# Placing the value products of two attention branches by TensorE's other work instead of by steps

## The chip, the cores and the metric

One NeuronCore of a Trainium2 chip runs the whole kernel in one launch. The metric is the device time of that launch in microseconds (us). A profiled execution leaves a trace with the time of each instruction on the five engines: TensorE (PE, with its weight loads as PEld), VectorE (DVE), ScalarE (ACT), GpSimd (POOL) and SyncE (SP), which here issues nearly all DMAs, in the order in which they stand on its queue.

## What is computed

The reference is one layer of a streaming encoder with two attention branches. 2048 new frames of one stream (and 128 of eight running streams, which a later part of the kernel serves from caches) are projected, go through both branches, and are merged. Cut to the parts that matter here:

```python
def diff_attention(q, k, v, qpos, kpos, lam):          # branch A: 4 heads of 128
    s = einsum('bhcqk', q, k) * (HEAD_DIM_A ** -0.5)   # c: two score maps
    p = softmax(where(chunk_mask, s, -inf), axis=-1)
    w = p[:, :, 0] - lam * p[:, :, 1]
    return einsum('bhqk,bkhe->bqhe', w, v)

def stick_breaking_attention(q, k, v, qpos, kpos):     # branch B: 8 heads of 64
    z = einsum('bhqk', q, k) * (HEAD_DIM_B ** -0.5)
    log_1m = where(kpos < qpos, log_sigmoid(-z), 0.)
    log_a = log_sigmoid(z) + reverse_cumsum(log_1m) - log_1m
    return einsum('bhqk,bkhd->bqhd', where(kpos < qpos, exp(log_a), 0.), v)
```

Both end in a product of attention weights with values. These value products are what the change moves.

## The kernel before

**Units and steps.** The attention part runs over 8 units, u = 0 to 7. Even units are one head of branch A, odd units two heads of branch B. A unit has 17 steps: first the tile of the running streams (`NT`, only projected here), then the tiles t = 0 to 15 of 128 queries each. Tile t attends to t + 1 blocks of 128 keys, so a step grows with t.

**What a step holds.** In step n the program writes out three streams. The first is a run of projection pieces (`project`, L430 and after: two 128x512 matmuls a piece at L445, for the gates at L521), which are some tiles ahead of the attention. The second is the scores of tile t (`scores`, L651): a chunk is 128 queries by up to 512 keys, two matmuls into one of three PSUM banks `ps_s` (L661, L662) and on the diagonal a third that adds the mask (L665). The third is the value products. `interleave` (L95) spreads the streams evenly over the step. The order in which the program is written is then turned into an order for each engine by a scheduler that lets an instruction pass another one that would have to wait; the engines keep that order.

**From scores to weights.** In B, ScalarE takes two sigmoids of each chunk (L123), VectorE runs a scan over it (L638), which frees the PSUM bank; when a segment of up to eight key blocks is complete, GpSimd multiplies (L644), ScalarE makes a 16-bit copy (L594), VectorE the rest (L595). In A, VectorE evacuates the chunk with a running maximum (L580) and ScalarE takes the exponentials when all chunks of the tile are there. Both end in `turn` (L586): one DMA transpose on SP's queue (L602) writes the segment's weights, turned, into a buffer `wt`. There are five such buffers (`WT_BUFS`); the sixth transpose waits until the products of the first have been read. A unit of A makes 24 such segments, one of B 48, 288 in all.

**B's q and k** are turned by DMA transposes on the same queue (L542, L543), A's by TensorE (L547, L551).

**The value products** (`pv`, L725): for a key block, A takes three matmuls (L718, L719, L720), B two (L722, L723), with the turned weights as stationary operand. Those of step n are written out in step n + 2 (`PV_LAG` = 2), spread over the stretch 0.1 to 1.0 of that step (`V_LO`, `V_HI`), one block at a time among scores and projections.

Of the kernel before, what the change touches and what calls it, by code (L numbers as in the profile page):

```python
# [32 lines left out]
NT = SEQ // P  # L33
# [3 lines left out]
NEG = -3.0e38  # L37
STICK = 14
SEG = 8
PV_LAG = 2  # L40
WT_BUFS = 5
SC_BUFS = 6
V_LO, V_HI = 0.1, 1.0
W_READY = 9
WIDE_BUFS = 6
P0_AT = 2.0, 4.0, 6.0
# [45 lines left out]
    return c  # L92


def interleave(*streams):  # L95

    order = []
    for i, pieces in enumerate(streams):  # L100
        lo, hi = 0.0, 1.0
        if isinstance(pieces, tuple):
            pieces, lo, hi = pieces
        total = sum(cost for cost, _ in pieces) or 1.0
        done = 0.0
        for j, (cost, fn) in enumerate(pieces):
            order.append((lo + (hi - lo) * (done + cost / 2) / total, i, j, fn))
            done += cost
    for _, _, _, fn in sorted(order, key=lambda e: e[:3]):
        fn()  # L110


# [1 line left out]
def layer_kernel(ctx: ExitStack, tc: tile.TileContext, a: dict):  # L114
# [81 lines left out]
    def bank(tag, dt=F32):  # L196
        return ps.tile([P, 512 if dt == F32 else 1024], dt, tag=tag, name=f"ps_{tag}", bufs=BANKS[tag])
# [98 lines left out]
    def split(hi, lo, src, s, on=None):  # L296

        if on is S:
            S.activation(out=hi, in_=src, func=AF.Identity, scale=s)  # L299
        elif on is G:  # L300
            G.tensor_scalar(out=hi, in0=src, scalar1=s, scalar2=0.0, op0=ALU.mult, op1=ALU.add)
        else:
            V.tensor_scalar(out=hi, in0=src, scalar1=s, scalar2=None, op0=ALU.mult)
        V.scalar_tensor_tensor(out=lo, in0=src, scalar=s, in1=hi, op0=ALU.mult, op1=ALU.subtract)
# [282 lines left out]
    def turn(job, seg, scale=None):  # L587

        nb = seg["hi"] - seg["lo"]
        nk = nb * P  # L590
        w16 = seg["n"].bitcast(F16)
        hi, lo, src = w16[:, 0:nk], w16[:, nk : 2 * nk], seg["p"][:, 0:nk]
        if scale is None:
            S.copy(out=hi, in_=src)  # L594
            V.tensor_tensor(out=lo, in0=src, in1=hi, op=ALU.subtract)  # L595
        else:
            split(hi, lo, src, scale, S)
        if job["t"] == NT:
            seg["wt"] = job["pool"].tile([P, 10, P], F16, tag="dwt", name="dwt", bufs=2)
        else:  # L600
            seg["wt"] = wtp.tile([P, 2 * SEG, P], F16, tag="wt", name="wt", bufs=WT_BUFS)
        nc.sync.dma_start_transpose(out=seg["wt"][:, 0 : 2 * nb, :], in_=w16[:, 0 : 2 * nk])  # L602

    def softmax_pair(job):

        segs = job["segs"]
        nm = tiny.tile([P, 2], F32, tag="nm", name="nm")
        V.tensor_reduce(out=nm, in_=job["mx"][:, :, 0 : job["nch"]], axis=AX.X, op=ALU.max, negate=True)
        l = tiny.tile([P, 2, 2], F32, tag="l", name="l")
        for i, seg in enumerate(segs):  # L610
            nk = (seg["hi"] - seg["lo"]) * P
            for c in range(2):
                w = seg[("p", "n")[c]][:, 0:nk]
                act(out=w, in_=w, func=AF.Exp, bias=nm[:, c : c + 1], accum_out=l[:, c, i : i + 1])
        r = tiny.tile([P, 3], F32, tag="r", name="r")
        sums = l[:, :, 0]
        if len(segs) > 1:
            V.tensor_tensor(out=sums, in0=l[:, :, 0], in1=l[:, :, 1], op=ALU.add)
        V.reciprocal(out=r[:, 0:2], in_=sums)
        V.scalar_tensor_tensor(out=r[:, 2:3], in0=sums[:, 0:1], scalar=r[:, 1:2], in1=nlam, op0=ALU.mult, op1=ALU.mult)  # L620
        V.tensor_tensor(out=r[:, 0:1], in0=r[:, 0:1], in1=ls[:, 0:1], op=ALU.mult)
        for seg in segs:
            nk = (seg["hi"] - seg["lo"]) * P
            p, n = seg["p"][:, 0:nk], seg["n"][:, 0:nk]
            V.scalar_tensor_tensor(out=p, in0=n, scalar=r[:, 2:3], in1=p, op0=ALU.mult, op1=ALU.add)
            turn(job, seg, r[:, 0:1])
# [81 lines left out]
    def store(U, t, o):  # L708
        ui = (U["h"] + 4 * U["kind"]) * P
        if U["kind"] == 0:  # L710
            sum_squares(o, P, osums[:, t, U["h"] : U["h"] + 1])
        load(out=o_d[t][:, ui : ui + P], in_=o)

    def pv_block(job, seg, po, wj, vt, first, last):

        wt, nb, c = seg["wt"], seg["hi"] - seg["lo"], job["c"]
        if job["U"]["kind"] == 0:
            T.matmul(po[:, 0:P], wt[:, wj, :], vt[:, :, 0, :], start=first, stop=False)  # L718
            T.matmul(po[:, 0:P], wt[:, wj, :], vt[:, :, 1, :], start=False, stop=False)  # L719
            T.matmul(po[:, 0:P], wt[:, nb + wj, :], vt[:, :, 0, :], start=False, stop=last)  # L720
        else:
            T.matmul(po[:, c * P : (c + 1) * P], wt[:, wj, :], vt[:, c, :, :], start=first, stop=False)  # L722
            T.matmul(po[:, c * P : c * P + 64], wt[:, nb + wj, :], vt[:, c, 0, :], start=False, stop=last)  # L723

    def pv(job):  # L725

        U, t, c = job["U"], job["t"], job["c"]
        segs = job["segs"] if U["kind"] == 0 else job["segs"][::-1]
        order = [(seg, j) for seg in segs for j in range(seg["hi"] - seg["lo"])]

        def block(i):
            seg, j = order[i]
            if i == 0 and (U["kind"] == 0 or c == 0):
                U["po", t] = bank("o")
            pv_block(job, seg, U["po", t], j, U["v"][seg["lo"] + j], i == 0, i == len(order) - 1)
            if i == len(order) - 1 and (U["kind"] == 0 or c == 1):
                store(U, t, natural(U, t, U.pop(("po", t))))

        return [(1.5, lambda i=i: block(i)) for i in range(len(order))]

    def cache_column(name, h):
        return "ab".index(name[0]) * 4 + h
# [167 lines left out]
    steps = [(u, t) for u in range(8) for t in [NT] + list(range(NT))]  # L910
    back = []
    spare, cached = norms()
    jobs = []


    line = []
# [32 lines left out]
    def position(x):  # L949

        m = min(int(x), len(steps) - 1)
        return starts[m] + (starts[m + 1] - starts[m]) * (x - m)

    def take(target, need):

        i = at[0]
        out = []
        while i < len(line) and (i < target or any(m <= need for m, _ in line[i : i + 14])):
            out.append((1.0, line[i][1]))
            i += 1  # L960
        at[0] = i
        return out
# [7 lines left out]
    def duration(t):  # L970
        return SAMPLE_TIME if t == NT else TILE_TIME + (t + 1) / 4
# [3 lines left out]
    with tc.tile_pool(name="p0", bufs=1) as p0:  # L975
# [5 lines left out]
        def wide_tile():  # L981
            return p0.tile([P, KT, 256], F32, tag="wide", name="wide", bufs=WIDE_BUFS)
# [21 lines left out]
        first = wide_tile().rearrange("p k n -> p (k n)")  # L1004
# [207 lines left out]
    cuts = None  # L1212
# [98 lines left out]

        return [branch_weight for _ in branch_weights] + [rest] + [lambda t=t: first(t) for t in tiles[0:2]]

    for n in range(len(steps) + PV_LAG):
        made, qk, vs = [], [], []
        if n < len(steps):
            u, t = steps[n]
            past += duration(t)
            if t == (3 if u == 0 else NT) and u < 7:
                back += prepare_unit(u + 1)  # L1320
            if u == 7 and not back and not spare and not cached and len(branch_weights) > 1:
                branch_weight()
            for fn in back[: -(-len(back) // max(1, (W_READY if u else W_READY + 2) - t % NT))]:
                back.pop(0)()
            for todo, here in ((spare, norm_at), (cached, keys_at)):
                if todo and here(u, t):
                    left = sum(here(*step) for step in steps[n:])
                    for _ in todo[: -(-len(todo) // left)]:
                        todo.pop(0)()
            if t < NT:  # L1330
                qk = scores(units[u], t, made)
        if n >= PV_LAG:
            for job in jobs[n - PV_LAG]:
                vs += pv(job)
        target = position(len(steps) * past / whole + LEAD)
        pieces = take(target, min(n + 1, len(steps) - 1))
        if at[0] == len(line) and not pieces and not spare and not cached:
            if cuts is None:
                cuts = early_work()
            pieces = [(1.0, fn) for fn in cuts[: -(-len(cuts) // (len(steps) + PV_LAG - n))]]  # L1340
            del cuts[: len(pieces)]
        interleave(pieces, qk, (vs, V_LO, V_HI))
        jobs.append(made)
    c01.close()


    with ExitStack() as c2:
# [7 lines left out]
        vs = scales(total(add_up_all(csums), 8), res, "s_c", 8)  # L1355
# [147 lines left out]
```

## Time and profile before

| what | value |
|---|---|
| median of 3 runs | 2333.5 us (2331.74 to 2335.74) |
| the profiled execution, its own time | 2332.17 us |
| its span in the trace | 2330.4 us |
| TensorE busy | 2089.3 us, 90% |
| VectorE, ScalarE, GpSimd busy | 1695.3, 1618.7, 693.9 us |
| mean granted TensorE clock | 0.961 |

The span is the time from the first to the last instruction of the trace; the execution's own time is 1.8 us longer. Busy time of TensorE is the union of its matmuls, whose ends are modelled. An idle time is put down to what ended it: "PE ps_o L722 <- DMA wt<-sc_n" is time in which TensorE stood before a value product of B until the transposed weights had landed.

### The profile page before, as it was taken

Reading aid. Unit: us, or ns where it says so; the run is one execution under the profiler, and the core shown is the slowest. Engines: PE = TensorE matmul, PEld = TensorE weight load, DVE = VectorE, ACT = ScalarE, POOL = GpSimd, SP = SyncE. Lnnn points to the kernel's source line nnn. Section 1 sums busy time; section 2 is a strip of 40 time slices with the busy share of each in tenths; the row PEclk is TensorE's granted clock in tenths of the full one; section 3 lists DMA queues with packets and bytes.
Section 4 is the critical chain, followed back from the end, with each engine's and each line's share of the span. In section 5 each row is a group of like instructions: output and inputs, shape, how many; then the busy total and the mean of one; then the engine's idle time right before and its main releaser. Section 6 shows DMA issues by size and latency. Waiting matters only on the chain. (4 is left out here: it accounts for less than half of the span.)

```text
span 2330.4 us, 41287 instructions
## 1 busy us (share of the span) xinstructions
PE 2089.3 (90%) x14344; PEld 1111.3 (48%) x14344; DVE 1695.3 (73%) x3659; ACT 1618.7 (69%) x3228; POOL 693.9 (30%) x610
## 2 busy tenths in 40 slices
PE   5998899988989888899998888999998688899998
PEld 3654454444545444455554444555454344344443
DVE  4658758669877776998668669777778768776763
ACT  4968767777877677878667777866778556555551
POOL 1222015346310333743024356401334312111211
PEclk7999999999999999999999999999998899899999
DMA  9777659898797899979889899676878899878431
GB/s 330 273 214 205 151 138 220 213 202 192 177 258 168 206 220 210 203 184 235 201 183 221 187 219 224 165 172 151 170 157 181 192 266 224 225 208 222 153 105 47
DMA packets 862402, 458.65 MB, mean 197 GB/s; under 512 B 593930, under 2 KB 801082, under 8 KB 861680
## 3 DMA queue, kind: packets, MB, share of 16 engines
q1 hardware_dynamic: 861244, 455.63, 80.6%
q8 instruction: 112, 1.84, 0.3%
q14 instruction: 98, 0.80, 0.1%
q10 hardware_dynamic: 948, 0.39, 0.1%
HBM read 228.82 MB, written 86.02 MB: 135 GB/s over the span
## 5 line engine op out<-in xcount | busy, mean ns | idle before, releaser
L644 POOL TENSOR_TENSOR sc_p<-sc_p,sc_n 128x127 f32<-128x127 f32 (+7 forms) x192 | 311.3, 1625 | 511.4 <-DVE sc_n L638 495.6
L445 PE MATMUL ps_mm<-wb,hs 128*128 128x512 f16 x1734 | 448.6, 385 | 4.6 <-DMA hs<-hT_d 4.6
L445 PEld LDWEIGHTS <-hs 128*128 128x128 f16 x3120 | 275.7, 99 | 263.6 <-DMA hs<-hT_d 12.7
L445 PE MATMUL ps_mm<-wa,hs 128*128 128x512 f16 x1386 | 349.0, 380 | 6.6 <-DMA hs<-hT_d 6.6
L661 PE MATMUL ps_s<-k,qst 128*128 128x512 f16 (+3 forms) x640 | 228.3, 357 | 72.3 <-DVE sc_n L638 57.5
L638 DVE TENSOR_TENSOR_SCAN sc_n<-ps_s,sc_n,zero_t 128x512 f32<-128x512 f32 x192 | 245.5, 1278 | 46.1 <-ACT ps_s L123 42.0
L595 DVE TENSOR_TENSOR sc_n<-sc_p,sc_n 128x128 f16<-128x128 f32 (+7 forms) x192 | 205.7, 1076 | 49.9 <-ACT sc_n L594 49.6
L521 PE MATMUL ps_t<-wb,hs 128*128 128x512 f16 x918 | 232.4, 380 | 0.0
L662 PE MATMUL ps_s<-k,qst 128*128 128x512 f16 (+3 forms) x640 | 228.0, 357 | 0.0
L722 PE MATMUL ps_o<-v,wt 128*128 128x128 f16 x1088 | 193.6, 228 | 37.9 <-DMA wt<-sc_n 37.8
L123 ACT ACTIVATE sc_p<-ps_s,usc 128x512 f32<-128x512 f32 (+3 forms) x320 | 204.4, 639 | 30.8 <-PE ps_s L662 17.2
L521 PEld LDWEIGHTS <-hs 128*128 128x128 f16 x1632 | 144.5, 99 | 140.5 <-issue 10.1
L594 ACT CAST sc_n<-sc_p 128x128 f16<-128x128 f32 (+7 forms) x192 | 154.3, 809 | 76.5 <-POOL sc_p L644 76.0
L123 ACT ACTIVATE ps_s<-ps_s,usc 128x512 f32<-128x512 f32 (+3 forms) x328 | 199.5, 608 | 0.0
L521 PE MATMUL ps_t<-wa,hs 128*128 128x512 f16 x714 | 187.7, 391 | 6.8 <-ACT qst L554 6.0
L1417 PE MATMUL ps_o<-wo,wa 128*128 128x512 f16 x816 | 182.8, 380 | 2.1 <-ACT wo L299 1.3
L723 PE MATMUL ps_o<-v,wt 128*128 128x64 f16 x1088 | 174.9, 200 | 0.0
L722 PEld LDWEIGHTS <-wt 128*128 128x128 f16 x1088 | 108.9, 103 | 120.7 <-DMA wt<-sc_n 46.6
L723 PEld LDWEIGHTS <-wt 128*128 128x128 f16 x1088 | 106.7, 102 | 73.1 <-issue 2.2
L580 DVE TENSOR_SCALAR_CACHE_REDUCE sc_n<-ps_s,usc 128x512 f32<-128x512 f32 (+3 forms) x160 | 106.3, 665 | 44.6 <-PE ps_s L665 21.7
L580 DVE TENSOR_SCALAR_CACHE_REDUCE sc_p<-ps_s,usc 128x512 f32<-128x512 f32 (+3 forms) x160 | 106.2, 664 | 26.4 <-PE ps_s L662 24.3
L718 PE MATMUL ps_o<-v,wt 128*128 128x128 f16 x544 | 105.0, 225 | 22.8 <-DMA wt<-sc_n 22.4
(365 smaller groups left out, 4346.4 us busy)
## 6 DMA issues: line engine op xcount, KB each, us to landing
hs<-hT_d SPq DMA_DIRECT2D x130, 512.0 KB, 4.5
g_d<-gt SPq DMA_DIRECT2D x68, 256.0 KB, 3.4
wb<-g_d SPq DMA_DIRECT2D x34, 512.0 KB, 5.3
out_dram<-pr SPq DMA_DIRECT2D x204, 64.0 KB, 2.3
wa<-in_w_in_dram SPq DMA_DIRECT2D x34, 256.0 KB, 3.9
o_d<-o SPq DMA_DIRECT2D x136, 64.0 KB, 2.6
hs<-o_d SPq DMA_DIRECT2D x17, 512.0 KB, 7.0
out_dram<-x SPq DMA_DIRECT2D x17, 512.0 KB, 2.8
```

The costliest lines, as they stand in the source:

```text
L123: i = S.activation(**kw)
L445: T.matmul(box["p"], box["h"][:, hi, k, :], U["w"][k][:, wi, :], start=(n == 0), stop=(n == 3 * KT - 1))
L521: T.matmul(box["g"][:, 0:gw], box["h"][:, hi, k, :], U["wg"][k // per][:, k % per, wi, :], start=(j == 0), stop=(j == 3 * KT - 1))
L580: V.tensor_scalar(out=dst[:, lo : lo + n], in0=p[:, 0:n], scalar1=sc_pos, scalar2=None, op0=ALU.mult, op1=ALU.max, accum_out=job["mx"][:, ...
L595: V.tensor_tensor(out=lo, in0=src, in1=hi, op=ALU.subtract)
L638: V.tensor_tensor_scan(out=dst[:, lo : lo + n][:, ::-1], data0=src[:, 0:n][:, ::-1], data1=zero_t[:, 0:1].to_broadcast([P, n]), initial=fi ...
L644: G.tensor_tensor(out=p[:, 0:m], in0=p[:, 0:m], in1=n[:, 1 : m + 1], op=ALU.mult)
L661: T.matmul(p[:, 0:n], qst[:, c, :], kk[:, c, 0:n], start=True, stop=False)
L662: T.matmul(p[:, 0:n], qst[:, 2 + c, :], kk[:, c, 0:n], start=False, stop=not diag)
L722: T.matmul(po[:, c * P : (c + 1) * P], wt[:, wj, :], vt[:, c, :, :], start=first, stop=False)
L723: T.matmul(po[:, c * P : c * P + 64], wt[:, nb + wj, :], vt[:, c, 0, :], start=False, stop=last)
L1417: T.matmul(po, st["y"][:, yi * 8 + k, :], wo[j * 4 + k // 2][:, wi, k % 2, :], start=(n == 0), stop=(n == 3 * KT - 1))
```

## The change

`pv` is no longer called two steps later. `turn` calls it for one segment right after it has written out that segment's transpose, and puts the segment's blocks into a list `due`, each with the mark `spent + 30.0`. `spent` adds up the estimated TensorE time of all that has been written out: 0.44 for a projection piece, 0.22 times its weight for a score chunk, 0.17 for a block of A, 0.085 for one of B. `give` writes out pieces and scores in the evenly mixed order, and after each of them all products whose mark has been reached. All blocks of a segment have the same mark, so they come in one run, where before they were spread over a step. At the end of the attention part what is left in `due` is mixed with the last pieces. The order of the blocks within a tile, the instructions and their number, the buffers and the PSUM banks are the same.

```diff
-PV_LAG = 2
+PV_LAG = 30.0
+PIECE, CHUNK, PV_A, PV_B = 0.44, 0.22, 0.17, 0.085
-V_LO, V_HI = 0.1, 1.0
...
         nc.sync.dma_start_transpose(out=seg["wt"][:, 0 : 2 * nb, :], in_=w16[:, 0 : 2 * nk])
+        if job["t"] < NT:
+            cost = (PV_A, PV_B)[job["U"]["kind"]]
+            due.extend((spent[0] + PV_LAG, cost, fn) for fn in pv(job, seg))
...
-    def pv(job):
+    def pv(job, seg):
...
-        return [(1.5, lambda i=i: block(i)) for i in range(len(order))]
+        return [lambda j=j: block(j) for j in range(nb)]
+
+    def give(order, costs):
+
+        for i, weight, fn in order:
+            fn()
+            spent[0] += weight * costs[i]
+            while due and due[0][0] <= spent[0]:
+                _, cost, product = due.pop(0)
+                product()
+                spent[0] += cost
...
-        if n >= PV_LAG:
-            for job in jobs[n - PV_LAG]:
-                vs += pv(job)
...
+            if n == len(steps) + 1:
+                pieces += [(PV_B / PIECE, fn) for _, _, fn in due]
+                due.clear()
-        interleave(pieces, qk, (vs, V_LO, V_HI))
-        jobs.append(made)
+        give(interleaved(pieces, qk), (PIECE, CHUNK))
```

Lines after the change stand a few lower: the products of B are L726 and L727, their transposes L603, the load of a tile's input L423.

**TensorE, the first products of tile 1 in unit 3 (B).** `wt` are the turned weights, `v` the values, `ps_o` the output's bank; `qst` and `k` belong to the scores of tile 2, `hs` is the input of a projection. Before:

```order
L662 LDWEIGHTS qst_8779
L662 MATMUL ps_s_9229<-k_8515,qst_8779 128x384
L665 LDWEIGHTS idb_194
L665 MATMUL ps_s_9229<-masks_196,idb_194 128x128
L722 LDWEIGHTS wt_9137
L722 MATMUL ps_o_9308<-v_8396,wt_9137 128x128
L723 LDWEIGHTS wt_9137
L723 MATMUL ps_o_9308<-v_8396,wt_9137 128x64
```

After:

```order
L522 LDWEIGHTS hs1_181
L522 MATMUL ps_t_9447<-wb1_1427,hs1_181 128x512
L726 LDWEIGHTS wt_9083
L726 MATMUL ps_o_9502<-v_8404,wt_9083 128x128
L727 LDWEIGHTS wt_9083
L727 MATMUL ps_o_9502<-v_8404,wt_9083 128x64
```

The products stood right behind the scores of tile 2; now they stand among the projections of a later tile. Between the last score matmul of tile 1 and its first product there were 90 matmuls for the first head and 44 for the second; now there are 172 and 183.

**SP, the transposes of q for tile 9 in unit 3.** `wt` with 16 rows are weights of eight key blocks (of tile 7 here), with 2 rows of one block (tile 8); `k` and `qst` are the keys and queries of tile 9. Before:

```order
L602 DMA_TRANSPOSE wt_9877<-sc_n_9841 128x16x128
L602 DMA_TRANSPOSE wt_9939<-sc_n_9906 128x16x128
L602 DMA_TRANSPOSE wt_10034<-sc_n_9980 128x2x128
L525 DMA g_d9_105<-gt0_1421 128x512
L542 DMA_TRANSPOSE k_9920<-k16_9965 128x2x128
L543 DMA_TRANSPOSE qst_10087<-qbuf1_214 128x4x128
```

After:

```order
L603 DMA_TRANSPOSE wt_9868<-sc_n_9825 128x16x128
L543 DMA_TRANSPOSE k_9914<-k16_9947 128x2x128
L716 DMA o_d5_67<-o_9985 128x128
L526 DMA g_d9_105<-gt0_1421 128x512
L544 DMA_TRANSPOSE qst_10083<-qbuf1_214 128x4x128
L603 DMA_TRANSPOSE wt_9931<-sc_n_9891 128x16x128
```

The queries stood behind three transposes of weights; now they stand behind one of these, and ahead of the second.

**SP, the weights of tiles 1 and 2 in unit 3.** `hs` are inputs of later projections, `wt` with 4 rows the weights of tile 1 (one for each head), with 6 rows those of tile 2. Before:

```order
L602 DMA_TRANSPOSE wt_9137<-sc_n_9130 128x4x128
L712 DMA o_d0_62<-o_9245 128x128
L501 DMA out_4_dram<-pr_9295 128x128
L602 DMA_TRANSPOSE wt_9161<-sc_n_9154 128x4x128
L502 DMA out_5_dram<-pr_9295 128x128
L422 DMA hs2_182<-hT_d1_58 128x2048
L542 DMA_TRANSPOSE k_9225<-k16_9298 128x2x128
L543 DMA_TRANSPOSE qst_9425<-qbuf1_214 128x4x128
```

After:

```order
L423 DMA hs2_182<-hT_d1_58 128x2048
L543 DMA_TRANSPOSE k_9168<-k16_9233 128x2x128
L544 DMA_TRANSPOSE qst_9396<-qbuf1_214 128x4x128
L423 DMA hs0_180<-hT_d2_59 128x2048
L603 DMA_TRANSPOSE wt_9107<-sc_n_9100 128x4x128
L526 DMA g_d5_101<-gt0_1421 128x512
L603 DMA_TRANSPOSE wt_9155<-sc_n_9148 128x6x128
L603 DMA_TRANSPOSE wt_9184<-sc_n_9177 128x6x128
```

The second head's weights of tile 1 stood ahead of the next input and of the keys and queries; now they stand behind them, and next to the weights of tile 2. The sixth transpose of weights waits for the products of the first, and those stand later than before.

More of the change, by code (lines that the diff above doesn't have):

```diff
@@ L92, in shape_constants, with interleaved @@
     return c
-def interleave(*streams):
+def interleaved(*streams):
     order = []
     for i, pieces in enumerate(streams):
-        lo, hi = 0.0, 1.0
-        if isinstance(pieces, tuple):
-            pieces, lo, hi = pieces
         total = sum(cost for cost, _ in pieces) or 1.0
@@ L106, in interleave @@
         for j, (cost, fn) in enumerate(pieces):
-            order.append((lo + (hi - lo) * (done + cost / 2) / total, i, j, fn))
+            order.append(((done + cost / 2) / total, i, j, cost, fn))
             done += cost
-    for _, _, _, fn in sorted(order, key=lambda e: e[:3]):
+    return [(i, cost, fn) for _, i, _, cost, fn in sorted(order, key=lambda e: e[:3])]
+def interleave(*streams):
+    for _, _, fn in interleaved(*streams):
         fn()
@@ L723, in pv_block, with block @@
             T.matmul(po[:, c * P : c * P + 64], wt[:, nb + wj, :], vt[:, c, 0, :], start=False, stop=last)
-    def pv(job):
[L727 to L733, printed above, removed]
+    due, spent = [], [0.0]
+    def pv(job, seg):
+        U, t, c, i = job["U"], job["t"], job["c"], job["segs"].index(seg)
+        last_seg = len(job["segs"]) - 1 if U["kind"] == 0 else 0
+        first_seg = 0 if U["kind"] == 0 else len(job["segs"]) - 1
+        nb = seg["hi"] - seg["lo"]
+        def block(j):
+            first, last = i == first_seg and j == 0, i == last_seg and j == nb - 1
+            if first and (U["kind"] == 0 or c == 0):
                 U["po", t] = bank("o")
-            pv_block(job, seg, U["po", t], j, U["v"][seg["lo"] + j], i == 0, i == len(order) - 1)
-            if i == len(order) - 1 and (U["kind"] == 0 or c == 1):
+            pv_block(job, seg, U["po", t], j, U["v"][seg["lo"] + j], first, last)
+            if last and (U["kind"] == 0 or c == 1):
                 store(U, t, natural(U, t, U.pop(("po", t))))
-        return [(1.5, lambda i=i: block(i)) for i in range(len(order))]
+        return [lambda j=j: block(j) for j in range(nb)]
[7 more added lines that the diff above has]
+                spent[0] += cost
     def cache_column(name, h):
@@ L1312, in early_work @@
         return [branch_weight for _ in branch_weights] + [rest] + [lambda t=t: first(t) for t in tiles[0:2]]
-    for n in range(len(steps) + PV_LAG):
-        made, qk, vs = [], [], []
+    for n in range(len(steps) + 2):
+        made, qk = [], []
         if n < len(steps):
@@ L1339, in layer_kernel @@
                 cuts = early_work()
-            pieces = [(1.0, fn) for fn in cuts[: -(-len(cuts) // (len(steps) + PV_LAG - n))]]
+            pieces = [(1.0, fn) for fn in cuts[: -(-len(cuts) // (len(steps) + 2 - n))]]
             del cuts[: len(pieces)]
-        interleave(pieces, qk, (vs, V_LO, V_HI))
-        jobs.append(made)
+            if n == len(steps) + 1:
+                pieces += [(PV_B / PIECE, fn) for _, _, fn in due]
+                due.clear()
+        give(interleaved(pieces, qk), (PIECE, CHUNK))
     c01.close()
```

1 line of the change is left out of this document (removed).

## The prediction

> **What bounds the kernel now.** I read the page's first rows, then the stretches of the span, then who waited for whom on TensorE, by unit, and last the timeline where the longest of these waits stand.
>
> ```profile
> span 2330.4 us, 41287 instructions
> PE 2089.3 (90%) x14344; PEld 1111.3 (48%) x14344; DVE 1695.3 (73%) x3659; ACT 1618.7 (69%) x3228; POOL 693.9 (30%) x610
> 140.00:1840.00 1700.00, 1538.61 (x10503) 825.79 (x10502) 1291.71 (x2648) 1270.71 (x2706) 582.45 (x506) 0.97 0.84 193
> ```
>
> TensorE is the busiest engine, and in the 1700 us of the attention part (third row: TensorE's 1538.61 us stand first after the length) it is idle for 161 us. No other engine comes near. So time is won where TensorE stops, unless the engine that feeds it has no room. Its stops, largest first:
>
> ```profile
> PE ps_s L661 <- DVE sc_n L638: 57.5, 54, 3.3
> PE ps_o L722 <- DMA wt<-sc_n: 37.8, 23, 4.8
> PE ps_o L718 <- DMA wt<-sc_n: 22.4, 18, 2.6
> ...
> PE ps_mm L445 <- DMA hs<-hT_d: 11.2, 5, 3.7
> ...
> PE ps_s L661 <- DMA qst<-qbuf: 4.2, 3, 1.9
> ```
>
> The columns are total, times, longest. Two waits carry the argument: 57.5 us before scores, until a scan has freed a PSUM bank, and 37.8 + 22.4 = 60.2 us before value products, until their weights have landed. The change aims at the second. 60.2 us is what it could win at most by its own means, and the place of each wait decides how much of it is real.
>
> The longest early wait of unit 3, in TensorE's timeline:
>
> ```profile
> 764.99 2.75 PE L445 MATMUL ps_mm<-wb,hs 128*128 128x512 f16 x12
> 767.58 1.46 PE L445 MATMUL ps_mm<-wa,hs 128*128 128x512 f16 x6
> ...
> 769.71 0.22 PE L665 MATMUL ps_s<-masks,idb 128*128 128x128 bf16 x1
> 773.31 0.23 PE L722 MATMUL ps_o<-v,wt 128*128 128x128 f16 x1 [3.37 <-DMA wt<-sc_n]
> ```
>
> and on SP's queue, the transposes of the same tile:
>
> ```profile
> 768.30 1.75 SPq L602 DMA_TRANSPOSE wt<-sc_n  x1
> ...
> 771.25 1.19 SPq L602 DMA_TRANSPOSE wt<-sc_n  x1
> ```
>
> The product stands in TensorE's order where its weights have only just been issued (768.30), and TensorE stops for 3.37 us with projections behind it that could have run. Twelve 128x512 matmuls take 767.58 - 764.99 = 2.59 us, 0.216 us each; this prices the distances that follow.
>
> **The change part by part.** No instruction is added or removed. The products themselves are as many as before, so their own time stays. What moves is their place.
>
> *1. Early tiles of B.* Counted in TensorE's order, from the last score matmul of a segment to its first product stand on average 106 matmuls in the tiles 0 to 7 of B before, and 179 after; for tile 1 of unit 3 it is 44 and 183 for the second head, of these 28 and 109 of 512 columns. At 0.216 us that is 6 us of wide matmuls before and 24 after. The waits at this place, unit 3 first, then unit 5 (stretches 760 to 845 and 1185 to 1275):
>
> ```profile
> PE ps_o L722 <- DMA wt<-sc_n: 4.6, 3, 3.4
> PE ps_o L722 <- DMA wt<-sc_n: 5.3, 2, 4.0
> ```
>
> All 4.6 + 5.3 = 9.9 us go, since 18 us of added work cover the longest of them four times. What is late next are the scores' banks: in the same stretch of unit 3 TensorE waits for the scan too.
>
> ```profile
> PE ps_s L661 <- DVE sc_n L638: 5.4, 6, 1.4
> ...
> 780.00:800.00 20.00, 18.49 (x119) 9.74 (x118) 16.03 (x32) 13.19 (x28) 9.49 (x8) 1.00 0.97 242
> 800.00:820.00 20.00, 18.66 (x119) 9.68 (x118) 15.70 (x25) 16.75 (x36) 9.99 (x10) 1.00 0.87 207
> 820.00:840.00 20.00, 15.71 (x96) 7.58 (x95) 18.67 (x22) 14.26 (x29) 9.68 (x8) 1.00 0.86 231
> ```
>
> VectorE (third busy time in a row) has 4 us of room in each 20 us until 820 and 1.3 us after that. So the gain lies between 0 (all of it is waited for again at the scan) and 9.9; I take two thirds, **-6.6 us**.
>
> TensorE's clock in that place is on record too:
>
> ```profile
> 760.00:780.00 20.00, 16.06 (x107) 8.62 (x105) 11.97 (x41) 13.16 (x35) 5.83 (x8) 0.91 0.77 182
> ```
>
> 0.91 of the clock was granted in the 20 us around the 3.37 us wait, 1.00 in the next three rows. The Trainium skill, page "TensorE: Matmul & The Clock Gate", section "HAM oscillation — how this bites in real kernels", says that an idle gap of more than about 3.4 us puts the array back to half rate for a window. By that rule each of the two longest early waits (3.4 and 4.0 us) also costs half a window, an estimate of 1.7 us, and the sum would be 3.4 us lower; the 0.91 agrees with it in size (0.09 of 20 us is 1.8 us).
>
> *2. Tiles of A.* The waits at A's products, in the stretches 134 to 330 (unit 0), 580 to 660 and 660 to 760 (unit 2), 1010 to 1075 and 1075 to 1185 (unit 4), 1500 to 1625 and 1625 to 1700 (unit 6):
>
> ```profile
> PE ps_o L718 <- DMA wt<-sc_n: 2.8, 2, 2.6
> PE ps_o L718 <- DMA wt<-sc_n: 2.5, 3, 1.2
> PE ps_o L718 <- DMA wt<-sc_n: 5.0, 3, 2.5
> PE ps_o L718 <- DMA wt<-sc_n: 1.4, 1, 1.4
> PE ps_o L718 <- DMA wt<-sc_n: 4.3, 3, 1.9
> PE ps_o L718 <- DMA wt<-sc_n: 2.7, 2, 1.9
> PE ps_o L718 <- DMA wt<-sc_n: 2.9, 2, 2.3
> ```
>
> In the order the distance grows from 111 to 148 matmuls in tiles 0 to 7 and from 148 to 176 in tiles 8 and 9, but at tile 11 of units 2 and 4 it is 183 before and 184 after, of these 105 and 100 wide ones. So the first, second, fourth and last row (2.8 + 2.5 + 1.4 + 2.9 = 9.6 us) go, and the rest (12.0 us) stays, most of it at tiles 10 and 11. There TensorE now arrives earlier by what units 2 and 4 had lost before it, 2.5 + 1.4 = 3.9 us, and waits that much more. Between 0 and 21.6 us, I take 9.6 - 3.9, **-5.7 us**.
>
> *3. Late tiles of B, and the end of unit 7.* In units 1, 3 and 5 the waits after tile 7 come to 2.6 + 1.1 + 3.5 us (stretches 410 to 580, 845 to 1010, 1275 to 1440), and at the end of unit 7 (1762 to 1840) to 20.6:
>
> ```profile
> PE ps_o L722 <- DMA wt<-sc_n: 2.6, 1, 2.6
> PE ps_o L722 <- DMA wt<-sc_n: 1.1, 1, 1.1
> PE ps_o L722 <- DMA wt<-sc_n: 3.5, 4, 1.5
> PE ps_o L722 <- DMA wt<-sc_n: 20.6, 12, 4.8
> ...
> 1800.00:1820.00 20.00, 10.76 (x89) 6.32 (x89) 19.48 (x21) 17.99 (x29) 12.49 (x7) 0.79 0.65 125
> ```
>
> The distance in tiles 12 to 15 of units 1, 3 and 5 is 183 and 181 matmuls, so the 7.2 us may go or double: **0**, between -7 and +7. At the end of unit 7 no projection is left to put between; VectorE is busy 19.48 of 20 us and sets the pace: **0**.
>
> *4. SP's queue in late B.* A segment's buffer comes free after its last block. Before, eight blocks were spread over several us of other work; now they come in one run. SP's transposes stood waiting for products, in the whole span and (second row) in the late half of unit 3, 860 to 1010:
>
> ```profile
> SPq L602 <- PE ps_o L723: 65.5, 30, 5.1
> SPq L602 <- PE ps_o L723: 14.4, 6, 2.9
> ```
>
> Everything behind them on the queue is held too: inputs, keys and queries of B. The queries of tile 9 move ahead of two such transposes. What TensorE sees of that is the 4.2 us before scores until queries landed, and a part of the scan's waits, where ScalarE had been held by a late load. I take half of the first, **-2.1 us**; between 0 and 14 us (4.2, and three units with one scan wait of the longest kind, 3.3).
>
> *Sum.* The profiled execution took 2332.2 us, 1.8 us more than its span. 2332.2 - 6.6 - 5.7 - 2.1 = 2317.8. The median of the runs is 1.3 us above the profiled one, so I forecast **2319 us**.
>
> **The rivals.** *The wait moves to the scan.* TensorE gets past the products and stands before the scores instead, because ScalarE and VectorE make no chunk sooner. For it: the 57.5 us are spread over 54 waits, in every unit of B, and in late B there is no room:
>
> ```profile
> 960.00:980.00 20.00, 16.23 (x138) 9.15 (x136) 19.24 (x20) 18.83 (x36) 14.15 (x11) 1.00 1.04 209
> ```
>
> Against it: the two terms that carry the sum lie where VectorE has 4 us in 20 to spare, or in A. With terms 1 and 2 given back, 2333.5 - 2.1 = **2331 us**, which I count as no change. The Trainium skill, page "Perfetto Trace Analysis", section "Optimization Strategy", says that the same bubble repeating on the engine that should be saturated can mean too little PSUM for the next tile; by that rule the 57.5 us want more banks, the change doesn't touch them, and the time would be the rival's.
>
> *The five buffers.* This one ends slower. Products of B's tiles 1 to 4 now come some 18 us later, while weights are made every few us, so the sixth transpose finds no buffer and SP's queue stands. The order shows it: the second head's weights of tile 1 move behind the next inputs and queries, beside those of tile 2. Price: eight transposes a unit, four units, each held as long as the longest such wait, 32 x 5.1 = 163 us on SP. Before, TensorE saw 11.2 + 4.2 us (inputs and queries) of 65.5 us on SP, 0.24 of it; 163 x 0.24 = 39 us. 2319 + 39 = **2358 us**. It decides as soon as the hold exceeds what inputs and queries have in hand; it eats the whole gain from 63 us of added waiting on SP (15 / 0.24). Against it: inputs and queries stand ahead of the held transposes in the new order, and a product that waits is far from its weights now.
>
> *That it doesn't do what it says* shows only in late A, where the distances in the order do not grow; that is in term 2.
>
> **How the numbers follow.** Forecast 0.60, the scan 0.20, the five buffers 0.20. Downwards the bounds of the terms add up to 9.9 + 9.6 + 7.2 + 14 = 41 us, all of which at once is unlikely: the low end is 2296. Upwards, half of the slower rival's size is taken in: 2345. About 0.12 is left above and 0.05 below. A measurement of this kernel tells 0.2% (4.7 us) from no change. Faster 0.64 (the forecast and a little of the scan case), within 0.2% 0.16, slower 0.20.
>
> **What would show it.** In the profile after, L726 waits for `wt` should be gone in tiles 0 to 7 of units 3 and 5, L722's gone in A but for tiles 10 and 11, the 20.6 us at the end still there, and TensorE's wait for the scan at most 5 us up. SP's L603 waits for products should rise in tiles 1 to 4 of B and fall in 9 to 13. The prediction is wrong if the scan's waits grow by as much as the products' fall, or if waits for `hs` and `qst` grow from 15 us by tens.

## The result, and the profile after

The changed kernel takes **2313.8 us** (median of 6 runs, 2307.88 to 2317.01) against 2333.3 us for the kernel before beside it: a ratio of 0.9915, with a 95% interval of 0.990 to 0.9929. That is 19.5 us less; 14.5 were forecast, and the time lies in the range. The reasons did worse than the number. Most of the gain came from unit 0, for which the prediction had 2.8 us inside a term, and for another cause.

The profiled execution took 2317.0 us. From the page after: the span, the busy times, and TensorE in the attention part (the first busy time after the length).

```profile
span 2315.2 us, 41268 instructions
PE 2087.2 (90%) x14344; PEld 1114.4 (48%) x14344; DVE 1693.4 (73%) x3659; ACT 1621.8 (70%) x3228; POOL 694.9 (30%) x610
140.00:1840.00 1700.00, 1551.11 (x10553) 835.66 (x10552) 1302.56 (x2674) 1278.41 (x2708) 587.00 (x507) 0.96 0.85 195
```

TensorE is idle for 148.9 us of these 1700, where it was 161.4. (The window is the same for both; after the change the last product ends 11 us earlier, so 11 us more of what follows lie in it.) The waits that the prediction went by, after the change:

```profile
PE ps_s L665 <- DVE sc_n L642: 56.4, 37, 8.5
PE ps_o L722 <- DMA wt<-sc_n: 23.7, 14, 2.6
PE ps_o L726 <- DMA wt<-sc_n: 21.8, 11, 6.9
PE ps_mm L446 <- DMA hs<-hT_d: 7.6, 4, 3.1
...
PE ps_s L665 <- DMA qst<-qbuf: 5.2, 4, 2.6
```

Before products of B (L726) 21.8 us are left of 37.8; before products of A (L722) 23.7 of 22.4, so nothing went. The scan's waits are as they were (57.5), fewer and longer. Inputs and queries cost 12.8 us for 15.4.

Where TensorE's idle time went shows by unit: a stretch runs from a unit's first score to the next unit's, and its length less TensorE's busy time is the idle time. The two last columns are the first two experiments below. The last stretch ends with TensorE's last matmul, 10.5 us before the end of the span.

| stretch | before | after | unit 0 alone new | all but unit 0 new |
|---|---|---|---|---|
| ahead of unit 0 | 26.5 | 28.1 | 27.8 | 28.1 |
| unit 0 (A) | 18.4 | **5.4** | 5.1 | 17.9 |
| unit 1 (B) | 26.0 | 24.7 | 25.5 | 23.3 |
| unit 2 (A) | 11.6 | 15.4 | 11.3 | 13.1 |
| unit 3 (B) | 28.1 | 24.1 | 27.1 | 25.7 |
| unit 4 (A) | 8.1 | 14.0 | 9.5 | 15.6 |
| unit 5 (B) | 28.7 | 25.1 | 26.4 | 21.8 |
| unit 6 (A) | 9.7 | 9.5 | 8.1 | 9.2 |
| unit 7 (B) | 30.9 | 28.9 | 31.4 | 33.6 |
| behind the last product | 42.7 | 42.2 | 39.0 | 40.6 |
| sum | 230.7 | 217.4 | 211.2 | 228.9 |

Unit 0 has 13.0 of the 13.3 us. The other units cancel: B's gain 10.9, A's units 2 and 4 lose 9.7. Unit 0 before and after, as one stretch each:

```profile
134.00:314.00 180.00, 161.59 (x1079) 87.43 (x1077) 125.63 (x355) 126.97 (x286) 27.07 (x34) 0.95 0.74 191
```

```profile
134.00:291.00 157.00, 151.58 (x1030) 81.96 (x1027) 125.79 (x347) 121.11 (x278) 32.17 (x35) 1.00 0.84 215
```

It is 23 us shorter: 13.0 of idle time and 161.59 - 151.58 = 10.0 of busy time. Little of the 10.0 us is work that only moved: between the first scores of units 0 and 1 stand 45 products and 6 transposes fewer and 6 projections more. At the spacing of an unhindered run (0.056 us for the products behind 251.02 us in the timeline of before, 0.216 for a projection) that is 51 x 0.056 - 6 x 0.216 = 1.6 us. The rest, some 8 us, goes with TensorE's rate: the granted clock is 0.95 in the first row and 1.00 in the second, and 0.05 of 180 us is 9 us. Over the whole span most of this part is lost again: units 2, 4 and 7 were granted 0.99, 0.99 and 0.91 before and 0.97, 0.95 and 0.88 after, and TensorE's busy time is only 2.1 us less. Unit 0's waits before:

```profile
PE ps_t L521 <- ACT qst L554: 6.0, 1, 6.0
PE ps_t L547 <- ACT qst L554: 3.7, 2, 3.5
PE ps_o L718 <- DMA wt<-sc_n: 2.8, 2, 2.6
PE ps_s L661 <- DVE sc_p L580: 2.5, 3, 2.0
PE ps_s L661 <- ACT qst L554: 1.5, 1, 1.5
PE ps_s L661 <- DVE sc_n L580: 1.4, 4, 0.7
```

and after:

```profile
PE ps_o L722 <- DMA wt<-sc_n: 4.8, 3, 2.5
...
```

11.2 us of the waits were for ScalarE's copies of turned queries (L554), and they are gone; the waits for weights, at which the change aims, have grown from 2.8 to 4.8 us. What has changed is TensorE's order. So many projection matmuls (without the gates') + products stand between the first score of a tile of unit 0 and that of the next:

| tile | 4 | 5 | 6 | 7 | 8 | 9 | 10 | 11 | 12 |
|---|---|---|---|---|---|---|---|---|---|
| before | 81+45 | 0+0 | 0+0 | 26+0 | 70+63 | 0+27 | 0+0 | 0+0 | 15+63 |
| after | 27+3 | 18+15 | 17+12 | 24+15 | 40+18 | 12+45 | 26+9 | 8+43 | 24+5 |

As written, both programs have 16 to 40 projections in each of these steps; it is the scheduler that packed the projections and the products before into three clumps, with tiles of scores between them that have nothing to hide behind. The third clump's foot in TensorE's timeline before, and ScalarE's:

```profile
237.38 0.27 PE L547 MATMUL ps_t<-id,k 128*128 128x128 f16 x2 [3.53 <-ACT qst L554]
...
243.85 3.17 PE L521 MATMUL ps_t<-wa,hs 128*128 128x512 f16 x7 [5.98 <-ACT qst L554]
246.81 0.63 PE L661 MATMUL ps_s<-k,qst 128*128 128x512 f16 x1
247.24 0.64 PE L662 MATMUL ps_s<-k,qst 128*128 128x512 f16 x1
247.66 1.57 PE L521 MATMUL ps_t<-wa,hs 128*128 128x512 f16 x5
249.07 1.46 PE L521 MATMUL ps_t<-wb,hs 128*128 128x512 f16 x6
250.37 0.38 PE L661 MATMUL ps_s<-k,qst 128*128 128x512 f16 x1
```

```profile
232.27 0.60 ACT L554 COPY qst<-ps_t 128x512 f16<-128x512 f16 x1
232.75 1.17 ACT L123 ACTIVATE sc_p<-sc_p,nm 128x1024 f32<-128x1024 f32 x1
...
236.72 0.60 ACT L554 COPY qst<-ps_t 128x512 f16<-128x512 f16 x1
...
243.18 0.62 ACT L554 COPY qst<-ps_t 128x512 f16<-128x512 f16 x1
```

The copies come 4.5 and 6.5 us apart, since ScalarE does a tile's exponentials (L123) between them. The transposes have one PSUM bank, `ps_t`, which is free only when the copy is done. TensorE has no projection and no product to do in between, and what stands next in its order, the next tile's transposes (L547) and then the gates' projections (L521), needs the same bank: it stands 3.53 and 5.98 us.

### The profile page after: what moved, and what is told of

Its sections match the earlier page's. It is cut to its first block, busy times and chain, and to the rows that moved or that the text cites. A ratio compares the mean times of both kernels' runs of the same rounds, so it can differ in the third digit from the quotient of the medians.

```text
span 2315.2 us, 41268 instructions
## 1 busy us (share of the span) xinstructions
PE 2087.2 (90%) x14344; PEld 1114.4 (48%) x14344; DVE 1693.4 (73%) x3659; ACT 1621.8 (70%) x3228; POOL 694.9 (30%) x610
## 5 line engine op out<-in xcount | busy, mean ns | idle before, releaser
L648 POOL TENSOR_TENSOR sc_p<-sc_p,sc_n 128x127 f32<-128x127 f32 (+7 forms) x192 | 303.7, 1586 | 544.1 <-DVE sc_n L642 500.9
L446 PEld LDWEIGHTS <-hs 128*128 128x128 f16 x3120 | 296.5, 99 | 335.9 <-issue 15.9
L446 PE MATMUL ps_mm<-wb,hs 128*128 128x512 f16 x1734 | 430.0, 382 | 3.1 <-DMA hs<-hT_d 2.5
L665 PE MATMUL ps_s<-k,qst 128*128 128x512 f16 (+3 forms) x640 | 228.8, 358 | 75.7 <-DVE sc_n L642 56.4
L522 PEld LDWEIGHTS <-hs 128*128 128x128 f16 x1632 | 155.4, 99 | 173.5 <-issue 6.1
L124 ACT ACTIVATE sc_p<-ps_s,usc 128x512 f32<-128x512 f32 (+3 forms) x320 | 202.4, 632 | 37.4 <-PE ps_s L666 25.5
L522 PE MATMUL ps_t<-wb,hs 128*128 128x512 f16 x918 | 226.0, 381 | 0.0
L522 PE MATMUL ps_t<-wa,hs 128*128 128x512 f16 x714 | 178.1, 383 | 0.0
L726 PE MATMUL ps_o<-v,wt 128*128 128x128 f16 x1088 | 130.9, 230 | 22.1 <-DMA wt<-sc_n 21.8
L642 DVE TENSOR_TENSOR_SCAN sc_n<-ps_s,zero_t 128x128 f32<-128x128 f32 (+3 forms) x128 | 103.8, 813 | 34.6 <-ACT ps_s L124 33.8
L726 PEld LDWEIGHTS <-wt 128*128 128x128 f16 x1088 | 105.0, 104 | 49.1 <-DMA wt<-sc_n 27.6
L487 POOL TENSOR_TENSOR rot<-pr,rope 128x256 f32<-128x256 f32 x68 | 60.6, 892 | 220.5 <-ACT pr L460 191.4
L1432 PEld LDWEIGHTS <-wa 128*128 128x128 f16 x816 | 78.4, 98 | 99.7 <-issue 6.4
```

The source lines that it names most:

```text
L124: i = S.activation(**kw)
L446: T.matmul(box["p"], box["h"][:, hi, k, :], U["w"][k][:, wi, :], start=(n == 0), stop=(n == 3 * KT - 1))
L522: T.matmul(box["g"][:, 0:gw], box["h"][:, hi, k, :], U["wg"][k // per][:, k % per, wi, :], start=(j == 0), stop=(j == 3 * KT - 1))
L642: V.tensor_tensor_scan(out=dst[:, lo : lo + n][:, ::-1], data0=src[:, 0:n][:, ::-1], data1=zero_t[:, 0:1].to_broadcast([P, n]), initial=fi ...
L648: G.tensor_tensor(out=p[:, 0:m], in0=p[:, 0:m], in1=n[:, 1 : m + 1], op=ALU.mult)
L665: T.matmul(p[:, 0:n], qst[:, c, :], kk[:, c, 0:n], start=True, stop=False)
```

## The experiments

Each ratio is to the kernel before on the same chip, with its 95% interval. In a mixed kernel, units outside `NEW` have their products written two steps after their scores, as before. All compute the same. Lines stand a few lower in the mixed kernels: A's products begin at L727, B's at L731, the copies of turned queries are L560. Stretches are read from one trace of each kernel; the traces come from several chips, on which the kernel before took 2333 to 2340 us, so that a few us between two traces show nothing.

**Unit 0 alone, and all but unit 0.**

```diff
+NEW = (0,)
...
-        if job["t"] < NT:
+        if job["t"] < NT and job["U"]["u"] in NEW:
...
+            for job in jobs[n - 2]:
+                if job["U"]["u"] not in NEW:
+                    segs = job["segs"] if job["U"]["kind"] == 0 else job["segs"][::-1]
+                    vs += [(1.5, fn) for seg in segs for fn in pv(job, seg)]
...
-        give(interleaved(pieces, qk), (PIECE, CHUNK))
+        give(interleaved(pieces, qk, (vs, V_LO, V_HI)), (PIECE, CHUNK, PV_A / 1.5))
```

> Unit 0 alone is placed the new way; in units 1 to 7 the products stand two steps after their scores, as before. In the traces of before and after, TensorE's idle time in unit 0 falls from 18.4 to 5.4 us, and 11.2 us of that are waits for ScalarE's copies of turned queries, which the prediction did not name; in the other units the changes (-1.3, +3.8, -4.0, +5.9, -3.6, -0.2, -2.0) cancel. Theory 1, unit 0's order: the whole gain comes from here, since the score tiles of unit 0 no longer stand in clumps of three with nothing between; this kernel takes 2314 to 2320 us, and the waits for the queries' copies in unit 0 are gone. Theory 2, the prediction's: the gain is in the early tiles of B; here only the 2.8 us of waits for weights in unit 0 can go, so 2330 to 2333 us.

The complement has `NEW = (1, 2, 3, 4, 5, 6, 7)`.

> The complement: unit 0 placed as before, units 1 to 7 the new way. Theory 1 (unit 0's order): nothing is left of the gain, 2330 to 2336 us (the idle changes of units 1 to 7 and the rest sum to -0.3 us), and the waits for the queries' copies (11.2 us) are there again in unit 0. Theory 2 (early tiles of B): most of the gain stays, 2314 to 2320 us.

Measured: 0.9903 (0.9885 to 0.9922) and 0.9987 (0.9973 to 1.0001). TensorE's waits in unit 0, alone and in the complement:

```profile
PE ps_o L727 <- DMA wt<-sc_n: 4.4, 2, 2.3
...
```

```profile
PE ps_t L527 <- ACT qst L560: 6.0, 1, 6.0
PE ps_t L553 <- ACT qst L560: 3.4, 1, 3.4
PE ps_o L727 <- DMA wt<-sc_n: 3.0, 1, 3.0
```

Unit 0's new placement alone gives the whole gain, and without it none is left that can be told from nothing. In the complement the early waits of units 3 and 5 are gone as well; it does not help.

**B alone.** `NEW = (1, 3, 5, 7)`.

> All units of B (1, 3, 5, 7) placed the new way, all units of A (0, 2, 4, 6) as before. Theory 1 with the trace's sums by unit: B's own units lost 1.3 + 4.0 + 3.6 + 2.0 = 10.9 us of idle time, so 2322 us, and units 2 and 4 stay at 11.6 and 8.1 us of idle time. Theory 2 (terms 1 and 4 of the prediction): 2324 us. If the 9.7 us that units 2 and 4 had more were work that B's new order pushed into them, they are there here as well: 2330 us or more.

**Unit 0 and B.** `NEW = (0, 1, 3, 5, 7)`.

> Unit 0 and all units of B the new way; units 2, 4 and 6 of A as before. If unit 0 and B's early tiles each carry their own gain and A's later units only lose by the change (idle +3.8, +5.9, -0.2), this is the fastest: 2333 - 13 - 11 = 2309 us, under the changed kernel's 2313.8. If A gains by the change as term 2 of the prediction has it (-5.7), it is slower than the changed kernel by some of that: 2317 to 2320 us.

Measured: 1.0099 (1.0076 to 1.0122) and 1.0017 (1.0002 to 1.0031), both slower than the two theories had them; the third possibility for B alone, work pushed into A's units, came nearest. Most of the loss is not in B's units, which in the first are 7 us longer together, but in units 2 and 4, which are 11.0 and 15.2 us longer (in the second 9.6 and 11.8). TensorE's waits in unit 2 of the first:

```profile
PE ps_o L727 <- DMA wt<-sc_n: 11.9, 6, 4.6
PE ps_s L670 <- DVE sc_p L586: 4.2, 2, 3.0
...
```

In the order a new clump stands there: 145 products behind the first score of tile 6, none behind those of tiles 1, 2, 3 and 5. Such a clump at a seam of two placements could be taken away by itself:

**B alone, without the seam.** What is due of B is written ahead of A's first products.

```diff
                 if job["U"]["u"] not in NEW:
+                    vs += [(1.5, fn) for _, _, fn in due]
+                    due.clear()
```

> B alone the new way, as in the kernel that took 2360 us, but whatever of B is still due is written ahead of A's first products. In the order this takes away the 145 products that stood in one stretch behind the first score of tile 6 in units 2 and 4. Theory 1 (a clump in A's early tiles is what costs): units 2, 4 and 6, which were 11.0, 15.2 and 3.7 us longer, come back to within some 4 us each; 2333 to 2343 us. If B's own new placement costs (buffers, SP's queue, banks), it stays at 2353 us or more.

Measured: 1.0004 (0.9994 to 1.0014). The 145 products are gone from the order and 22 us from the time; units 2 and 4 are 4.3 and 4.4 us longer than before, unit 6 3.7 shorter. So taking the clump away gave back 6.7, 10.8 and 7.4 us in the three units: it costs there too. B's own new placement, now without unit 0's help, gives nothing, as in the complement above.

**Distance or run?** In unit 0 only, all blocks of a tile in one run, at the old distance:

```diff
+                    blocks = [fn for seg in segs for fn in pv(job, seg)]
+                    if job["U"]["u"] == 0:
+                        vs.append((1.5 * len(blocks), lambda blocks=blocks: [fn() for fn in blocks]))
```

> As before in all units, but in unit 0 all blocks of a tile are written in one run in the middle of the step, two steps after the scores: the run without the distance. In TensorE's order unit 0 keeps its clumps (behind the first score of tile 4 stand 81 projections and 45 products, between those of tiles 5, 6 and 7 none). Theory 1a (the distance opens the clumps): no gain, 2329 to 2337 us, and 9 to 13 us of waits for ScalarE's copies of turned queries in unit 0. Theory 1b (products that run together keep banks and copies free): a gain of ten us or more, 2314 to 2323 us.

And unit 0 only (`NEW = (0,)`), with `PV_LAG = 10.0`:

> Unit 0 alone the new way, with a distance of 10 in place of 30; units 1 to 7 as before. The order then is even up to tile 7, but before tiles 11 and 12 no projection is left, and 99 products stand behind the first score of tile 12. Theory 1 (evenness of the order in unit 0): the first half of the gain comes, the second (the 9.7 us of waits for the queries' copies at tile 12 in the trace of before) does not: 2320 to 2328 us, between before and the kernel with 30. Were it enough that products follow pieces at all, it would take 2311 to 2317 us; were it the landing of weights, TensorE would wait in unit 0 for weights, 10 us or more.

Measured: 1.0003 (0.9991 to 1.0016) for the one run, whose waits in unit 0 are those of before:

```profile
PE ps_t L527 <- ACT qst L560: 5.9, 1, 5.9
PE ps_t L553 <- ACT qst L560: 4.5, 3, 3.5
PE ps_o L727 <- DMA wt<-sc_n: 4.2, 4, 2.8
```

The run is not what opens the clumps. The distance of 10 gave 0.9907 (0.9894 to 0.992), more than expected: on the scale of 2333 us it is 2312, and 2320 to 2328 was written. Its unit 0 is only part of the way, as its order said: 9.6 us idle, with the third clump still there.

```profile
PE ps_s L670 <- DVE sc_p L586: 5.6, 2, 5.3
PE ps_o L727 <- DMA wt<-sc_n: 2.2, 3, 0.8
```

The rest lies behind the attention. The kernel with one run, which was run beside it on the same chip and has the old order in units 2 to 6 and behind the last product, is the one to measure against: of the 24.6 us between the two spans (2341.4 and 2316.8 us) 12.7 lie in unit 0 and 10.6 between the last product and the end (495.5 and 484.9 us). That last stretch is 494.2 us before, 489.5 in the changed kernel, 486.7 with unit 0 alone and 486.3 in its complement; its first 220 us are in another order in all of these but the kernel with one run. It was shorter in the complement too, which gained nothing as a whole. I had no term for that either, and no run takes it apart.

**45 in units 1 to 7.** Unit 0 stays at 30.

```diff
-            due.extend((spent[0] + PV_LAG, cost, fn) for fn in pv(job, seg))
+            due.extend((spent[0] + (PV_LAG if job["U"]["u"] == 0 else 45.0), cost, fn) for fn in pv(job, seg))
```

> Unit 0 with 30 as in the changed kernel, units 1 to 7 with 45. In TensorE's order A's products then stand 26 to 42 us of TensorE's work behind their scores in units 2, 4 and 6 (18 to 28 with 30). If A's waits for weights stayed because 30 as written is only 18 to 28 us in the order, 15 of the 23.7 us go: 2298 to 2306 us. The five buffers (the prediction's slower rival): with up to 42 us a buffer is held over two and a half late tiles of A, two buffers a tile, so SP's waits for products go up from 46 to over 80 us, waits for inputs and queries up from 13 by 10 or more, and the time is 2318 us or more.

Measured: 1.0089 (1.0074 to 1.0104). The waits for weights are gone in units 2, 4 and 6, all 20.8 us (18.2 before products of A, 2.6 before products of B), and the time is 41 us above the changed kernel's. The waits point at the five buffers. SP, VectorE and TensorE of this kernel, the row of each that matters (lines here and in the last run are those of the changed kernel: L726 and L727 are B's products):

```profile
SPq L603 <- PE ps_o L727: 79.8, 44, 4.0
```

```profile
DVE sc_n L641 <- DMA wt<-sc_n: 104.5, 36, 6.5
```

```profile
PE ps_s L665 <- DVE sc_n L642: 90.5, 73, 6.8
```

SP's transposes wait for products (41.8 us with 30), score buffers whose transposes are held stay occupied, VectorE waits 104.5 us for them at L641 (2.5 us with 30), its scans are late, and TensorE stands before the scores for 90.5 us. The units of B are 10 to 23 us longer than before. No run has more buffers, so the chain is read from these waits and not tested by itself.

**45 or 40 for A only, and 45 for A with B as before.** The mark's `45.0` only where `kind` is 0 and the unit isn't 0; then `40.0`; then the first with `NEW = (0, 2, 4, 6)`.

> A's units 2, 4 and 6 with 45, unit 0 and all of B with 30. In the trace of the kernel with 45 everywhere, TensorE's waits for weights are gone from units 2, 4 and 6 (20.8 us in the changed kernel), and their idle time is 32.2 us against 38.9; the loss was in B (scan waits up, VectorE waiting for score buffers whose transposes stood on SP). Theory: what 45 costs is a matter of B's many short tiles, so here A's gain of 7 us stays and B is as in the changed kernel: ratio to before 0.987 to 0.990, 2304 to 2310 us on the scale of 2333.5. Rival: B's first products now queue behind A's last ones (35 to 39 us of TensorE's work behind their scores in tiles 0 and 1 of unit 3, 25 with 30), buffers are held there and B loses 10 us or more: ratio 0.994 or above.

> The same with 40 for A's units 2, 4 and 6. By the theory of the run with 45 it has most of A's gain (26 to 31 us behind the scores in tiles 1 to 12 of unit 2) and less of the queueing in B: ratio 0.987 to 0.991. If the buffers decide, it lies between the changed kernel (0.9915) and the run with 45.

> Unit 0 with 30, units 2, 4 and 6 with 45, and all of B placed as before, two steps behind. If the gain of unit 0 (ratio 0.9903 alone) and A's 45 (20.8 us of waits for weights, of which 7 us of idle time are a gain) add up, 0.986 to 0.989, 2301 to 2308 us. If A's late products collide with B's first, written two short steps behind their scores, a clump forms at the start of units 3, 5 and 7 and it is above 0.992.

Measured: 0.9921 (0.9906 to 0.9936), 0.993 (0.9912 to 0.9949) and 0.9918 (0.9903 to 0.9934): none better than the changed kernel (nor can unit 0 alone, 0.9903, be told from it). In the first the waits for weights are gone in units 2 and 4, but their idle time is 13.4 and 11.2 us against 15.4 and 14.0, since other waits came in their place, and unit 7, where all later things meet, is 10 us longer than in the changed kernel.

**15 everywhere.** `PV_LAG = 15.0`.

> All units with 15 in place of 30. The prediction's first term says that the early tiles of B gain from 30: with 15 their waits for weights return, some 7 us, ratio 0.994 or above (2319 us or more). By the order of unit 0 (uneven from tile 10 on, as in the run with a distance of 10 in unit 0 alone, ratio 0.9907) and the small weight of units 1 to 7 (ratio 0.9987 without unit 0), it takes what the changed kernel takes, 0.989 to 0.993.

Measured: 1.0081 (1.0068 to 1.0095), 39 us above the changed kernel; my theory of unit 0 had it equal, and it is refuted in that form; the prediction's first term, 0.994 or above, was on the right side.

```profile
PE ps_o L726 <- DMA wt<-sc_n: 52.3, 45, 6.2
PE ps_o L722 <- DMA wt<-sc_n: 38.7, 22, 5.9
PE ps_s L665 <- DVE sc_n L642: 35.2, 32, 2.9
```

91.0 us of waits for weights where 30 has 45.5; of the 45.5 us more, 21.2 are had back at the scan. Not all of the loss is by weights: of the 37 us between the two spans 14 are in unit 0, where the third clump is back in the order (no projection behind the first scores of tiles 10 and 11, 99 products behind that of tile 12), 10 in unit 3 and 6 in unit 6, while units 1, 2 and 4 differ by about 1 us at most. That units 1 to 7 give nothing between "two steps" and 30, and lose both at 15 and at 45, would fit a best distance between those two; that is argued from three settings and not shown.

## Why the prediction was right and wrong

The time fell into the range, 5 us from the forecast, but that is luck to a good part: the two terms that carry the sum (-6.6 and -5.7 us) brought nothing when all units but unit 0 had the change, and the gain came from the order of unit 0, which neither of them counts.

*Early tiles of B* (-6.6 us): right at its place. No wait for `wt` is left in units 3 and 5, where 11.4 us were (9.9 in the stretches that were read), and the scan's waits there hardly moved. Unit 3 after:

```profile
PE ps_s L665 <- DVE sc_n L642: 17.1, 9, 6.3
PE ps_s L221 <- ACT junk L282: 2.7, 2, 2.2
...
```

The idle time of both units fell by 7.6 us. As a term of the sum it failed: "what is late next" was looked for in the same unit, and units 2 and 4 were idle for 9.7 us more. The run with all but unit 0 has these waits away and a ratio of 0.9987. The 3.4 us that the prediction priced for the clock in this place did not show either: units 3 and 5 were granted 0.98 and 0.97 before, 0.97 and 0.95 after.

*Tiles of A* (-5.7 us): wrong. "The distance grows", so 9.6 us were to go; A's products waited 22.4 us before and 23.7 after. Unit 2 before and after:

```profile
PE ps_o L718 <- DMA wt<-sc_n: 7.5, 6, 2.5
PE ps_o L722 <- DMA wt<-sc_n: 2.6, 1, 2.6
...
```

```profile
PE ps_o L722 <- DMA wt<-sc_n: 8.7, 5, 2.6
PE ps_s L665 <- DVE sc_n L581: 4.0, 1, 4.0
PE ps_mm L446 <- DMA hs<-hT_d: 2.0, 2, 1.6
```

I had counted how far the distance grew and not whether it was enough. The mark says 30 us, but in TensorE's order 18 to 28 us are left in units 2 and 4 (14 to 25 before); with 45 as written, 26 to 42, the waits are gone. The 4.0 us before a score and the 2.0 us for an input are new. Which of the two placements brings them is not separated: units 2 and 4 were idle for longer with B's new placement alone, and with A's alone at 45. The row of 2.9 us that the prediction gave to unit 6 and let go with the early tiles (1625 to 1700) lies behind the first score of unit 7, at 1608.6 us: these were products of unit 6's last tiles, so its reason does not hold for them, though that wait is gone.

*Unit 0* was 2.8 us in that term; 13.0 us of idle time came. The step that failed stands at its head: "What moves is their place", of the products alone. The comparison of the orders was made at products and transposes; projections, scores and the transposes of q move as well when a scheduler starts from another program. The 11.2 us of waits for copies stood in the trace of before, and the clumps in its order.

*Late B and the end of unit 7* (0): right; the wait at the end is 19.2 us for 20.6, and of the 7.2 us in units 1, 3 and 5 no wait is left there, 2.6 us a unit later.

*SP's queue* (-2.1 us): right in size by luck. SP waited 41.8 us for products in place of 65.5, less in tiles 9 to 13 of units 3 and 5 (8.8 and 13.9 us, now 7.1 and 8.8) and a little more in tiles 1 to 4, as said. But the term was taken from the queries, and they lost 1.0 us; the inputs, which it left out, gained 3.6.

*The rivals.* The wait did not move to the scan (56.4 us for 57.5). The five buffers cost nothing that shows at 30: SP's waits for products fell. At 45 the waits have their mark, and the price is near the one worked out (39 us, measured 41), which is luck too: it came by the score buffers and VectorE and not mainly by inputs and queries, and at another distance.

Why the scheduler makes clumps from one distance and not from another stays open: the runs show that they cost, and that a distance of 10 opens the first in unit 0.

## What to carry to other kernels

Where a scheduler decides the order, compare the whole order of the bounding engine before and after, not only the instructions that the edit names: count its filling work between the steps of the chain that paces it, and look for stretches without any. A distance between producer and consumer has two prices, the wait when it is short and the held buffers when it is long; here 15 and 45 each cost 40 us over 30, for 15 over a third of it in unit 0, where a clump came back, and of the 30 written in the program 18 to 28 were left in the order. A wait that is gone from a profile is a gain only if the span says so: undo the change one stage at a time before believing a table of waits. A stop of the bounding engine costs more than its own length when the engine runs slower behind it: look at the granted clock beside the idle time.

## What the runs showed of the hardware

TensorE's rate after a stop. In the rows of before shown above, the seven matmuls of 512 columns behind the gap of 5.98 us take 246.81 - 243.85 = 2.96 us, 0.42 each; the six at 249.07 take 1.30 us, 0.217 each. The granted clock in this stretch, before and after:

```profile
227.00:258.00 31.00, 20.17 (x144) 10.72 (x143) 24.00 (x68) 24.77 (x57) 0.03 (x1) 0.83 0.57 109
```

```profile
227.00:258.00 31.00, 31.00 (x213) 16.81 (x212) 24.41 (x64) 23.88 (x53) 0.00 (x0) 1.00 0.80 169
```

Up to 249.07 us 14 matmuls of 512 columns take 5.22 us, where 14 x 0.217 are 3.04: this stop is paid for a second time, by some 2.2 us. The Trainium skill, page "TensorE: Matmul & The Clock Gate", section "HAM oscillation — how this bites in real kernels", has half rate after a gap of more than about 3.4 us; the 0.42 against 0.217 us agree. As a limit the 3.4 us are not borne out here. Two other stops of the trace of before:

```profile
217.70 0.29 PE L718 MATMUL ps_o<-v,wt 128*128 128x128 f16 x1 [2.58 <-DMA wt<-sc_n]
217.78 0.32 PE L719 MATMUL ps_o<-v,wt 128*128 128x128 f16 x1
217.89 0.31 PE L720 MATMUL ps_o<-v,wt 128*128 128x128 f16 x1
...
929.26 0.38 PE L661 MATMUL ps_s<-k,qst 128*128 128x512 f16 x1 [3.29 <-DVE sc_n L638]
929.47 0.38 PE L662 MATMUL ps_s<-k,qst 128*128 128x512 f16 x1
```

After 2.58 us the products stand 0.11 us apart, double the 0.056 of an unhindered run; after 3.29 us the scores stand 0.21 us apart, which is the full rate. What decides between the two no run here shows.
